# First block's norm from feature-major x, the product chain opened ahead of the second value tiles, and weights split once and reloaded

## The chip, the core and the metric

The kernel runs on one core of one Trainium2 chip. The metric is device time in microseconds for one execution. The profile is of one execution, taken by the hardware profiler. PE is TensorE's matmul queue, PEld its weight loads, DVE is VectorE, ACT is ScalarE, POOL is GpSimd and SP is SyncE, whose queue issues nearly all DMAs here.

## The reference, cut to what matters

One layer of a hybrid encoder trunk over 2048 tokens of width 1024. A norm, one wide input projection, three groups of heads that read it (a banded softmax attention, an mLSTM and a gated linear attention, GLA), an output projection, a residual and a final norm.

```python
hn = rmsnorm(x, norm_g)                      # x * rsqrt(mean(x*x) + eps) * g
z = jnp.einsum('bsd,de->bse', hn, w_in)      # 1024 -> 4252 columns, split by group:
# aq ak av ag | mq mk mv mo mi mf mg | gq gk gv ga gg
y_a = band_chunk_attention(aq, ak, av, rel_bias) * silu(ag)
h_ml = mlstm_chunkwise(silu(conv(mq)), silu(conv(mk)), mv, mi + b_i, mf + b_f)
y_b = sigmoid(mo) * head_rmsnorm(h_ml, ml_norm_g) * silu(mg)
log_alpha = log_sigmoid(ga @ w_alpha + b_alpha) / 16
y_c = head_rmsnorm(gla_chunkwise(gq, gk, gv, log_alpha), gla_norm_g) * silu(gg)
x = x + concat(y_a, y_b, y_c) @ w_out        # then the final rmsnorm
```

Inside GLA the score of a token t against an earlier token j of its chunk is `sum_d q[t,d] * k[j,d] * exp(b[t,d] - b[j,d])`, with b the running sum of log_alpha: the decay differs by key channel.

## The kernel before, in words

**Two phases.** Phase A goes through the sequence in four blocks of 512 tokens (`for q in range(NQ)`, L753). For each block it makes all input projections, the mLSTM and the GLA; the q, k, v and gate of the attention, and the finished parts of y, go to DRAM scratch. Phase B (from L783) does the attention and the output projection. In phase B only the four last `a` projections of block 3, kept back by `proj_a` (L504), have to do with the change.

**Split products.** Each projection is done with numbers split in two: a high part, rounded to a 32-bit matmul format, and the remainder as low part. A tile pair of 128 contraction rows takes three matmuls, high by high, high by low and low by high (L243 to L245, L263 to L265). x is split once a block by `split_x` (L323, ACT L329 and DVE or POOL L330) into eight tiles `X[k]`. Weights are split each time that they are used, by `load_w` (L229): the raw tile (0.5 MB, two buffers `wraw`) is loaded from DRAM (L233), ACT rounds it (L235), and DVE or POOL subtracts (L236; every third goes to POOL, `other()` L128). The split tile, 1 MB, goes into a ring of five (`wring`, L138). A block uses 33 of them: 25 of feature-major projections (`proj_f`, 24 matmuls each, one weight) and 8 of the two value projections (`proj_t`, 96 matmuls and four weights each).

**The order of the work.** The order on TensorE is that in which the program is written (`manual_schedule`, L132); the other engines and the SP queue are ordered ahead of time by the framework's scheduler, and each works through its list in order. `high_priority(offset=AHEAD)` moves instructions forward in that scheduler. To fill TensorE's waits, the program weaves chains into the projections: `Flow` (L33) keeps a clock in microseconds; a chain is a generator that yields (its TensorE time, a pause); after every half of a projection (`flow.piece(12 * 0.227)`) each chain whose pause is over takes one step. `flow.need(name)` steps the chains until that one is finished, and emits no projection meanwhile.

**One block, in order** (L753 to L778): `proj_z` makes the GLA's q and k (gq, gk); `proj_v` makes the first value tiles, calls `proj_gg` for the GLA's gate, and then makes the second value tiles; `need("gates")`; the chains `gla_in` and `gla` start (L761, L762); `proj_m` makes the six mLSTM q and k tiles; the chain `mlstm` starts; `proj_gm` makes the mLSTM's gates; then, if there is a next block, `need("gla_in")` (L771), and the chain `prep` for the next block starts; `proj_a` makes the attention's tiles; `need("prep")`, `split_x`, and the chain `gates` of the next block starts.

**The chains.** `gates` (L334): gate rows, log-sigmoids, scans (DVE L349, L353), then the transposed rows `rt` and, last, the row `iwl` (L391). `gla_in` (L621): for each half of the block, exponentials of the decay sums, and then the products of each token with the earlier ones in its group of 16, on POOL (L649 scales, L652 multiplies into four buffers `prd`), summed over channels by matmuls that write the bank `pw` (L658); so four products, then PE, then four more. `gla` (L665): L688 to L692 and L709 to L716, the norm, and the transposes L739. `mlstm` (L520): for each of four chunks L531, L541 to L545, L559 to L576, the norm on POOL and DVE (L595 to L601), a pause of 9 us, a wait until the gates `gm` exist, the transposes L610, and the result to DRAM.

**The norm of x.** `prep_x` (L281) loads the block's four row-major tiles of x, squares them on ACT with a sum per row (L287), and makes the scale of each token: mean plus epsilon on DVE (L288), the power -0.5 on POOL (L289), and four diagonal matrices on DVE (L292). `prep` (L295) spreads the scale over all partitions by a matmul with ones (L299), copies it to SBUF (L301), loads the four feature-major tiles of x (L305), scales them on DVE (L308) and makes the gate inputs (L315, L320). For the first block both run before any projection (L748 to L751), after 14 warm-up matmuls (L154) and beside the making of constants (L174 to L213: the `zr` lines fill `hl_nm`, `hl_iw` and `sel`).

Of the kernel before, what the change touches and what calls it, by code (L numbers as in the profile page):

```python
# [16 lines left out]
P = 128  # L17
# [10 lines left out]
G0 = 96  # L28

# [70 lines left out]
def f32(ap):  # L100
    return ap.bitcast(FP32)
# [3 lines left out]
def trunk_kernel(ctx: ExitStack, tc: tile.TileContext, xT, x, w_f, w_t, w_o, w_gates, norm_g, conv_w,  # L105
# [11 lines left out]
    y_d = dram.tile([NQ, P, KT, QT], FP32, name="y_d")  # L117

# [9 lines left out]
    def other():  # L128
        turn["n"] += 1
        return nc.gpsimd if turn["n"] % 3 == 0 else nc.vector  # L130
# [11 lines left out]
    with ExitStack() as pa_:  # L142
# [6 lines left out]
        def bank(tag, n=1):  # L149
            return (psum_i if tag == "ip" else psum).tile([P, 512], FP32, name=tag, bufs=n)  # L150
# [5 lines left out]
        def d_tile():  # L156
            return big.tile([P, 6, L], FP32, name="dd", bufs=1)
# [17 lines left out]
        zr = d_tile()  # L175
        nc.gpsimd.memset(zr, 0.0)
        nc.vector.tensor_copy(hl_nm, zr.rearrange("p h t -> p (h t)")[:, 0:QT])
        nc.vector.tensor_copy(hl_iw, zr[:, 0, 0:NC])
        nc.gpsimd.affine_select(out=zr[0:32], in_=zr[0:32], pattern=[[-1, 6], [0, P]], compare_op=ALU.not_equal,
                                fill=1.0, base=0, channel_multiplier=1)  # L180
        nc.scalar.copy(zr[32:64], zr[0:32])
        nc.scalar.copy(zr[96:128], zr[0:32])
        nc.vector.memset(zr[0:32], 0.0)
        nc.vector.tensor_copy(sel, zr)
# [44 lines left out]
        def load_w(src, k):  # L229
            w = wring.tile([P, 2 * D], FR, name="w").rearrange("p (k l n) -> p k l n", k=k, l=2)  # L230
            with tc.high_priority(offset=AHEAD):
                raw = wraws.tile([P, D], FP32, name="wraw")
                nc.sync.dma_start(raw, src)  # L233
                rv = raw.rearrange("p (k n) -> p k n", k=k)
                nc.scalar.copy(w[:, :, 0, :], rv)  # L235
                other().tensor_tensor(w[:, :, 1, :], rv, f32(w[:, :, 0, :]), op=ALU.subtract)  # L236
            return w

        def proj_g(name, X, out_, per):
            w = load_w(w_f[_F.index(name)], KT)  # L240
            ps = bank("ip", 2)
            for k in range(KT):
                nc.tensor.matmul(ps, w[:, k, 0, :], X[k][:, 0, :], start=(k == 0), stop=False)  # L243
                nc.tensor.matmul(ps, w[:, k, 0, :], X[k][:, 1, :], start=False, stop=False)  # L244
                nc.tensor.matmul(ps, w[:, k, 1, :], X[k][:, 0, :], start=False, stop=(k == KT - 1))  # L245
                if k % per == per - 1:
                    yield
            out_.append(ps)
# [7 lines left out]
        def proj_t(j, X, evac):  # L256
            ws = [load_w(w_t[j, g], 2) for g in range(4)]
# [37 lines left out]
        def prep(q, R, dg):  # L295
            t0 = q * QT
            yield 0.0, 0.0
# [23 lines left out]
            R["raws"], R["g1"] = raws, g1  # L321

# [197 lines left out]
        def mlstm(q, qk, vs, R):  # L520
            rt, iwl = R["rt"], R["iwl"]
            for c in range(NC):
# [81 lines left out]
                yield 1.7, 9.0  # L604
# [16 lines left out]
        def gla_in(q, z, ls_all, G):  # L621
            NB = ST // 16
            for sub in range(2):
# [124 lines left out]
        flow.start("prep", prep(0, R, prep_x(0)))  # L748
        load_consts()
        flow.finish("prep")  # L750
        X = split_x(R["raws"])  # L751
        flow.start("gates", gates(0, R["g1"], R))
        for q in range(NQ):  # L753
# [3 lines left out]
            z = proj_z(X)  # L757
            vs, vg, gg = proj_v(X, lambda: proj_gg(X))
            flow.need("gates")
            G = {}  # L760
            flow.start("gla_in", gla_in(q, z, R["ls"], G))  # L761
# [349 lines left out]
```

## Time and profile before

| | us |
|---|---|
| three runs | 1397.63, 1402.09, 1406.93 |
| median | 1402.09 |
| the profiled execution | 1396.99 |
| its span, from the first instruction to the last | 1395.3 |
| PE busy in the span | 1308.3 |
| POOL busy | 609.2 |
| mean granted clock of TensorE | 0.958 |

The first projection matmul (L243) starts at 32.3 us. Block 0 lasts to about 270 us, blocks 1 and 2 about 240 us each; phase B starts at about 972 us. A stage row gives a stretch of time, its length, and the busy time (and number of instructions) of PE, PEld, DVE, ACT, POOL, then the granted clock, the busy share of the DMA engines and GB/s. A timeline row gives start, busy time, engine, line, operation, out and in, and in brackets the idle time before it and what ended it. A wait row gives who waited for whom, the total in us, how often, and the longest.

### The profile page before, as it was taken

The page shows a single profiled execution, that of the slowest core. Times are in us where ns is not written, and L with a number is a line of the kernel's source. Part 1 is how long each engine was busy: PE and PEld are TensorE (multiplying, and loading weights), DVE is VectorE, ACT ScalarE, POOL GpSimd, SP SyncE. Part 2 cuts the span into 40 slices and gives each one's busy share as a digit, 9 for nine tenths or more (in the row PEclk, how much of TensorE's full clock was granted, in tenths as well). Part 3 has the DMA queues.
Part 4 walks back from the last instruction along what each step waited for, and adds up shares of the span by engine and source line. Part 5 has one row for each costly group of instructions (what it writes and reads, how often), then busy time and mean ns, then how long its engine had stood idle before and what let it go on. Part 6 is the DMA issues. An engine that isn't in the chain of part 4 may idle for free.

```text
span 1395.3 us, 20018 instructions
## 1 busy us (share of the span) xinstructions
PE 1308.3 (94%) x7044; PEld 1060.7 (76%) x7044; DVE 809.1 (58%) x1886; ACT 602.4 (43%) x1149; POOL 609.2 (44%) x847
## 2 busy tenths in 40 slices
PE   4999999999998999999899999997968999999997
PEld 2787778788777878877688787886857877877876
DVE  7626566562856556474556547555657756756731
ACT  5634322563432365343135434221566645645631
POOL 4225752431665234277322526631354453453452
PEclk7999999999998999999899999996969999999999
DMA  7444224534322463422233542231596654554222
GB/s 247 141 134 135 76 71 140 190 114 136 106 77 66 135 236 90 142 87 81 75 106 117 144 151 91 82 110 49 164 274 182 183 157 149 164 170 153 78 76 84
DMA packets 107205, 180.10 MB, mean 129 GB/s; under 512 B 9824, under 2 KB 54752, under 8 KB 107104
## 3 DMA queue, kind: packets, MB, share of 16 engines
q1 hardware_dynamic: 102496, 170.43, 40.2%
q10 hardware_dynamic: 4608, 8.39, 1.6%
q8 instruction: 56, 0.92, 0.3%
q14 instruction: 45, 0.37, 0.1%
HBM read 143.14 MB, written 35.65 MB: 128 GB/s over the span
## 4 chain that ended last, share of the span: by engine, by line
PE 72%; DVE 11%; DMA 5%; ACT 4%; POOL 3%; issue 3%; SPq 1%; POOLq 0%; DVEq 0%; ACTq 0%
PE ip L243 12%; PE ip L245 11%; PE ip L244 11%; PE ip L263 3%; PE ip L265 3%; PE ip L264 3%; PE s L860 3%; PE ip L984 3%; PE ip L982 3%; PE ip L983 3%; PE tp L924 2%; DVE pt L874 2%; PE ga L692 2%; PE w L941 2%; DMA wraw<-in_w_o 2%
## 5 line engine op out<-in xcount | busy, mean ns | idle before, releaser
L243 PE MATMUL ip<-x,w 128*128 128x512 f32 x800 | 329.5, 412 | 0.0
L245 PE MATMUL ip<-x,w 128*128 128x512 f32 x800 | 314.4, 393 | 0.0
L244 PE MATMUL ip<-x,w 128*128 128x512 f32 x800 | 313.8, 392 | 0.0
L243 PEld LDWEIGHTS ip<-x,w 128*128 128x128 f32 x800 | 151.3, 189 | 45.6 <-issue 15.9
L245 PEld LDWEIGHTS ip<-x,w 128*128 128x128 f32 x800 | 151.3, 189 | 33.9
L244 PEld LDWEIGHTS ip<-x,w 128*128 128x128 f32 x800 | 151.8, 190 | 30.0 <-issue 2.6
L236 POOL TENSOR_TENSOR w<-wraw,w 128x1024 fp32r<-128x1024 f32 x44 | 106.2, 2413 | 149.1 <-ACT w L235 149.1
L235 ACT CAST w<-wraw 128x1024 fp32r<-128x1024 f32 x132 | 138.1, 1047 | 60.5 <-DMA wraw<-in_w_t 25.3
L236 DVE TENSOR_TENSOR w<-wraw,w 128x1024 fp32r<-128x1024 f32 x88 | 119.5, 1358 | 76.4 <-ACT w L235 74.9
L879 POOL TENSOR_SCALAR pt<-pt,sm 128x640 f32<-128x640 f32 (+2 forms) x96 | 70.5, 736 | 147.9 <-DVE sm L878 116.9
L982 PE MATMUL ip<-wo,y 128*128 128x512 f32 x256 | 106.7, 417 | 0.0
L263 PE MATMUL ip<-w,x 128*128 128x512 f32 x256 | 100.4, 392 | 3.6 <-ACT vg L426 3.5
L877 ACT ACTIVATE pt<-pt,sm 128x640 f32<-128x640 f32 (+2 forms) x96 | 73.3, 763 | 69.8 <-DVE sm L874 67.4
L984 PE MATMUL ip<-wo,y 128*128 128x512 f32 x256 | 101.4, 396 | 0.3 <-POOL y L890 0.3
L983 PE MATMUL ip<-wo,y 128*128 128x512 f32 x256 | 101.2, 395 | 0.0
L265 PE MATMUL ip<-w,x 128*128 128x512 f32 x256 | 99.7, 389 | 0.0
L264 PE MATMUL ip<-w,x 128*128 128x512 f32 x256 | 99.6, 389 | 0.0
L930 DVE TENSOR_TENSOR pl<-tp,ph 128x512 fp32r<-128x512 f32 (+2 forms) x126 | 74.6, 599 | 32.0 <-ACT ph L929 30.7
L860 PE MATMUL s<-kk,qq 128*128 128x384 f32 (+1 forms) x360 | 80.9, 334 | 12.4 <-DVE sm L874 10.7
L652 POOL TENSOR_TENSOR prd<-gk,zg 128x16 f32<-128x16 f32 (+15 forms) x128 | 72.2, 564 | 31.1 <-PE pw L658 24.5
L860 PEld LDWEIGHTS s<-kk,qq 128*128 128x128 f32 x360 | 60.6, 201 | 31.3 <-DVE sm L874 25.0
L929 ACT CAST ph<-tp 128x512 fp32r<-128x512 f32 (+2 forms) x126 | 63.0, 509 | 34.1 <-PE tp L924 33.3
(244 smaller groups left out, 2413.9 us busy)
## 6 DMA issues: line engine op xcount, KB each, us to landing
wraw<-in_w_f SPq DMA_DIRECT2D x100, 512.0 KB, 3.6
wraw<-in_w_t SPq DMA_DIRECT2D x32, 512.0 KB, 3.7
qq<-q_d SPq DMA_DIRECT2D x48, 256.0 KB, 4.3
kk<-k_d SPq DMA_DIRECT2D x18, 512.0 KB, 6.3
vv<-v_d SPq DMA_DIRECT2D x18, 512.0 KB, 7.1
xraw<-in_x SPq DMA_DIRECT2D x16, 512.0 KB, 5.0
xraw<-in_xT SPq DMA_DIRECT2D x16, 512.0 KB, 6.4
xr<-in_x SPq DMA_DIRECT2D x16, 512.0 KB, 3.7
```

The costliest lines, as they stand in the source:

```text
L235: nc.scalar.copy(w[:, :, 0, :], rv)
L236: other().tensor_tensor(w[:, :, 1, :], rv, f32(w[:, :, 0, :]), op=ALU.subtract)
L243: nc.tensor.matmul(ps, w[:, k, 0, :], X[k][:, 0, :], start=(k == 0), stop=False)
L244: nc.tensor.matmul(ps, w[:, k, 0, :], X[k][:, 1, :], start=False, stop=False)
L245: nc.tensor.matmul(ps, w[:, k, 1, :], X[k][:, 0, :], start=False, stop=(k == KT - 1))
L263: nc.tensor.matmul(ps, X[k][:, 0, t], w[:, 0, :], start=(k == 0), stop=False)
L264: nc.tensor.matmul(ps, X[k][:, 0, t], w[:, 1, :], start=False, stop=False)
L265: nc.tensor.matmul(ps, X[k][:, 1, t], w[:, 0, :], start=False, stop=(k == KT - 1))
L860: nc.tensor.matmul(sp[:, :cn], qq[:, l, tt * P:(tt + 1) * P], kk[:, ko + c0:ko + c0 + cn], start=(l == 0), stop=(l == 1))
L982: nc.tensor.matmul(ps, Y[k][:, 0, t], wo[k, j][:, 0, :], start=(e == 0), stop=False)
L983: nc.tensor.matmul(ps, Y[k][:, 0, t], wo[k, j][:, 1, :], start=False, stop=False)
L984: nc.tensor.matmul(ps, Y[k][:, 1, t], wo[k, j][:, 0, :], start=False, stop=(e == KT - 1))
```

## The change

It has three parts.

1. *First block.* `prep_first` takes the place of `prep_x(0)`, `prep(0)`, `split_x` and `proj_z` of block 0. It loads only the feature-major x, squares it on ACT, adds the two tiles of a pair on DVE, sums over partitions by one-column matmuls, makes the scale as before, and spreads it per 128 tokens into a PSUM bank that the scaling reads. The order on ACT, DVE, POOL and SP is fixed by `keep_in_program_order`. The loads of x, gq and gk are first on the SP queue; the constants' loads and the `zr` lines come later (`late_consts`). The products of gq and gk are ordered so that all that need only the high part of x come first; the gate inputs come between them and the rest.
2. *The chain.* `gla_in` starts after `proj_gg`, ahead of the second value tiles, and polls until `iwl` exists. `need("gates")` moves behind `proj_m`, `need("gla_in")` in the block goes, and `prep` polls until `gla_in` is over. The pause of the last mlstm chunk's result becomes 17 us in blocks 0 to 2.
3. *The weights.* `load_w` stores each split tile (1 MB) to DRAM scratch when it is first made; every later use loads the split tile back, with no raw tile, rounding or subtraction.

```diff
+    w_d = [dram.tile([P, 2 * D], FP32, name=f"w_d{i}") for i in range(len(_F) + 8)]
...
+        def load_w(src, k, i):
+            flat = wring.tile([P, 2 * D], FR, name="w")
+            w = flat.rearrange("p (k l n) -> p k l n", k=k, l=2)
             with tc.high_priority(offset=AHEAD):
+                if i in made:
+                    nc.sync.dma_start(f32(flat), w_d[i])
+                    return w
                 raw = wraws.tile([P, D], FP32, name="wraw")
                 nc.sync.dma_start(raw, src)
                 rv = raw.rearrange("p (k n) -> p k n", k=k)
                 nc.scalar.copy(w[:, :, 0, :], rv)
                 other().tensor_tensor(w[:, :, 1, :], rv, f32(w[:, :, 0, :]), op=ALU.subtract)
+            made.add(i)
+            nc.sync.dma_start(w_d[i], f32(flat))
             return w
...
         def prep(q, R, dg):
-            yield 0.0, 0.0
+            while "gla_in" in flow.chains:
+                yield 0.0, 1.0
...
+        def prep_first():
+            pin = tc.keep_in_program_order
+            with tc.high_priority(offset=2 * AHEAD):
+                for g in range(4):
+                    raw = xraws.tile([P, 2, QT], FP32, name="xraw")
+                    pin(nc.sync.dma_start(raw, xT[:, 2 * g:2 * g + 2, 0:QT]))
...
+                for g in range(4):
+                    sq = sqs[:, 2 * (g % 3):2 * (g % 3) + 2, :]
+                    pin(nc.scalar.activation(sq, raws[g], AF.Square))
+                    pin(nc.vector.tensor_tensor(sq[:, 0, :], sq[:, 0, :], sq[:, 1, :], op=ALU.add))
+                    for tt in range(NC):
+                        nc.tensor.matmul(ss[:, tt:tt + 1], sq[:, 0, tt * P:(tt + 1) * P], ones[:, 0:1], ...)
+                pin(nc.vector.tensor_scalar(rs, ss[:, 0:NC], 1.0 / D, EPS, op0=ALU.mult, op1=ALU.add))
+                pin(nc.gpsimd.tensor_tensor(rs, rs, mhalf[:, 0:NC], op=ALU.pow))
...
+                for tt in range(NC):
+                    pin(nc.vector.tensor_scalar(dg[:, tt, :], ident, rs[:, tt:tt + 1], None, op0=ALU.mult))
+                    nc.tensor.matmul(rb[:, tt * P:(tt + 1) * P], ones, dg[:, tt, :], start=True, stop=True)
...
+                for (w, wr), n in zip(ws, ("gq", "gk")):
+                    pin(nc.scalar.copy(w[:, :, 0, :], wr))
+                    pin(nc.gpsimd.tensor_tensor(w[:, :, 1, :], wr, f32(w[:, :, 0, :]), op=ALU.subtract))
+                    nc.sync.dma_start(w_d[8 + _F.index(n)], f32(w).rearrange("p k l n -> p (k l n)"))
...
+                for k in range(KT):
+                    pin(nc.vector.scalar_tensor_tensor(rk[k], rk[k], ng[:, k:k + 1], rb, op0=ALU.mult, op1=ALU.mult))
+                    last = [pin(nc.scalar.copy(X[k][:, 0, :], rk[k])).ins, None]
+                for k in range(KT):
+                    op = pin((nc.gpsimd if k in LO_POOL else nc.vector).tensor_tensor(X[k][:, 1, :], rk[k], f32(X[k][:, 0, :]), op=ALU.subtract))
...
+            load_consts()
+            late_consts(last)
...
-                yield 1.7, 9.0
+                yield 1.7, 9.0 if c < NC - 1 or q == NQ - 1 else 17.0
...
-        def gla_in(q, z, ls_all, G):
+        def gla_in(q, z, R, G):
             NB = ST // 16
+            while "iwl" not in R:
+                yield 0.0, 1.0
...
+            z = proj_z(X) if q else z
             G = {}
-            flow.start("gla_in", gla_in(q, z, R["ls"], G))
+
+            def between():
+                g = proj_gg(X)
+                flow.start("gla_in", gla_in(q, z, R, G))
+                return g
+
+            vs, vg, gg = proj_v(X, between)
             flow.start("gla", gla(q, vg, gg, G))
             flow.need("mlstm")
             if q + 1 < NQ:
                 dg = prep_x(q + 1)
             qk = proj_m(X)
+            flow.need("gates")
...
             if q + 1 < NQ:
-                flow.need("gla_in")
                 R = {}
                 flow.start("prep", prep(q + 1, R, dg))
```

More of the change, by code (lines that the diff above doesn't have):

```diff
@@ L28 @@
 G0 = 96
+LO_POOL = (4, 7)
+LO_ORDER = (0, 1, 2, 3, 5, 6, 4, 7)
 class Flow:
@@ L174, in trunk_kernel @@
         hl_iw = one.tile([P, NC], FR, name="hl_iw")
[L175 to L184, printed above, removed]
         cap = one.tile([P, L], FP32, name="cap")
@@ L226, in load_consts @@
             nc.vector.tensor_scalar(glg, glg, 0.5, None, op0=ALU.mult)
-        def load_w(src, k):
-            w = wring.tile([P, 2 * D], FR, name="w").rearrange("p (k l n) -> p k l n", k=k, l=2)
+        made = set()
+        def load_w(src, k, i):
+            flat = wring.tile([P, 2 * D], FR, name="w")
+            w = flat.rearrange("p (k l n) -> p k l n", k=k, l=2)
             with tc.high_priority(offset=AHEAD):
+                if i in made:
+                    nc.sync.dma_start(f32(flat), w_d[i])
+                    return w
                 raw = wraws.tile([P, D], FP32, name="wraw")
@@ L256, in proj_t @@
         def proj_t(j, X, evac):
-            ws = [load_w(w_t[j, g], 2) for g in range(4)]
+            ws = [load_w(w_t[j, g], 2, 4 * j + g) for g in range(4)]
             for tt in range(NC):
@@ L321, in prep, with late_consts @@
             R["raws"], R["g1"] = raws, g1
+        def late_consts(last):
+            zr = d_tile()
+            nc.gpsimd.memset(zr, 0.0)
+            with tc.issue_after(last[1]):
+                nc.vector.tensor_copy(hl_nm, zr.rearrange("p h t -> p (h t)")[:, 0:QT])
+            with tc.issue_after(last[1]):
+                nc.vector.tensor_copy(hl_iw, zr[:, 0, 0:NC])
+            nc.gpsimd.affine_select(out=zr[0:32], in_=zr[0:32], pattern=[[-1, 6], [0, P]], compare_op=ALU.not_equal,
+                                    fill=1.0, base=0, channel_multiplier=1)
+            with tc.issue_after(last[0]):
+                nc.scalar.copy(zr[32:64], zr[0:32])
+            with tc.issue_after(last[0]):
+                nc.scalar.copy(zr[96:128], zr[0:32])
+            with tc.issue_after(last[1]):
+                nc.vector.memset(zr[0:32], 0.0)
+            with tc.issue_after(last[1]):
+                nc.vector.tensor_copy(sel, zr)
@@ L619, in trunk_kernel @@
         b16 = lambda t: t.rearrange("p (b i) -> p b i", i=16)
-        def gla_in(q, z, ls_all, G):
+        def gla_in(q, z, R, G):
             NB = ST // 16
+            while "iwl" not in R:
+                yield 0.0, 1.0
+            ls_all = R["ls"]
             for sub in range(2):
@@ L747, in trunk_kernel @@
         R = {}
[L748 to L752, printed above, removed]
+        g1, X, z = prep_first()
+        flow.start("gates", gates(0, g1, R))
         for q in range(NQ):
@@ L756, in trunk_kernel @@
             flow.need("gla")
-            z = proj_z(X)
-            vs, vg, gg = proj_v(X, lambda: proj_gg(X))
-            flow.need("gates")
+            z = proj_z(X) if q else z
             G = {}
-            flow.start("gla_in", gla_in(q, z, R["ls"], G))
+            def between():
[3 more added lines that the diff above has]
+            vs, vg, gg = proj_v(X, between)
             flow.start("gla", gla(q, vg, gg, G))
```

52 lines of the change are left out of this document (51 added, 1 removed).

## The prediction

> **What bounds the kernel now.** I read the page first: engine shares, the sliced PE and clock rows, the chain that ended last.
>
> ```profile
> PE 1308.3 (94%) x7044; PEld 1060.7 (76%) x7044; DVE 809.1 (58%) x1886; ACT 602.4 (43%) x1149; POOL 609.2 (44%) x847
> ...
> PEclk7999999999998999999899999996969999999999
> ...
> PE 72%; DVE 11%; DMA 5%; ACT 4%; POOL 3%; issue 3%; SPq 1%; POOLq 0%; DVEq 0%; ACTq 0%
> ```
>
> TensorE is the bound nearly everywhere. Only the places where it isn't can pay, and the dips of the clock row point at them. A table by stage (us; then busy time of PE, PEld, DVE, ACT, POOL; granted clock, DMA share, GB/s) has the stages cut where the matmuls of the projections stop and start again:
>
> ```profile
> 0.00:32.30 32.30, 14.50 (x46) 7.47 (x46) 23.21 (x53) 17.89 (x25) 16.98 (x27) 0.74 0.76 252
> ...
> 179.90:194.10 14.20, 11.48 (x86) 8.86 (x85) 9.56 (x25) 4.21 (x9) 12.83 (x25) 0.76 0.26 75
> ...
> 418.00:433.80 15.80, 11.90 (x86) 8.69 (x85) 8.81 (x22) 4.21 (x9) 13.47 (x24) 0.68 0.19 54
> ...
> 654.50:671.00 16.50, 11.80 (x85) 8.92 (x84) 9.97 (x26) 4.21 (x9) 13.46 (x25) 0.79 0.20 53
> ...
> 937.20:971.70 34.50, 24.66 (x164) 22.44 (x163) 21.01 (x67) 5.70 (x13) 8.12 (x19) 0.71 0.14 36
> ```
>
> So there are five holes: the start, three equal stretches of 14.2, 15.8 and 16.5 us in which TensorE issues only some 86 small matmuls while POOL is the busy engine (12.8 to 13.5 us), and the end of the first phase. The three are the line that drains the product chain, `flow.need("gla_in")`, L771: nothing of the projections may be issued until the last products (POOL L649/L652) are summed (PE L658). What TensorE waited for between 32 and 937 us says the same, and names the rest:
>
> ```profile
> PE pw L658 <- POOL prd L652: 6.2, 5, 1.8
> PE mt L610 <- DVE m L601: 5.4, 2, 3.7
> ...
> PE ip L263 <- ACT vg L426: 3.5, 3, 2.0
> ```
>
> No projection matmul waited for a weight tile in that list.
>
> **Part 1, the first block.** Landings, single steps and the first matmuls in the order of time:
>
> ```profile
> 4.38 1.04 ACT L235 CAST w<-wraw 128x1024 fp32r<-128x1024 f32 x1 [2.31 <-DMA wraw<-in_w_f]
> ...
> 5.69 1.04 ACT L235 CAST w<-wraw 128x1024 fp32r<-128x1024 f32 x1 [0.26 <-DMA wraw<-in_w_f]
> ...
> 8.84 1.06 ACT L287 ACTIVATE xraw<-xraw 128x1024 f32<-128x1024 f32 x1 [2.10 <-DMA xraw<-in_x]
> ...
> 15.22 1.03 POOL L289 TENSOR_TENSOR rs<-rs,mhalf 128x4 f32<-128x4 f32 x1 [4.27 <-DVE rs L288]
> ...
> 16.29 0.87 DVE L292 TENSOR_SCALAR g<-ident,rs 128x128 f32<-128x128 f32 x4 [1.15 <-POOL rs L289]
> ...
> 27.67 1.28 DVE L330 TENSOR_TENSOR x<-xraw,x 128x512 fp32r<-128x512 f32 x2
> ```
> ```profile
> 17.30 2.04 PE L299 MATMUL pw<-g,ones 128*128 128x512 f32 x2 [10.36 <-DVE g L292]
> ...
> 32.32 0.50 PE L243 MATMUL ip<-x,w 128*128 128x512 f32 x1
> ```
> ```profile
> 44.20 0.39 PE L245 MATMUL ip<-x,w 128*128 128x512 f32 x1
> ...
> 45.11 0.39 PE L263 MATMUL ip<-w,x 128*128 128x512 f32 x1
> ```
>
> The two first weight loads land 1.31 us apart, 0.524 MB each: 400 GB/s. Four matmul starts lie between 44.20 and 45.11, so a projection matmul costs 0.2275 us. The first value tile starts at 45.11.
>
> Removed: four row-major x loads ahead of four more of feature-major x, and the wait between the two. In the new order the four feature-major loads are first on the SP queue: landed at 4.4, 5.7, 7.0, 8.3, and gq and gk at 9.6 and 10.9. Then in a row: last square 1.06, pair sum 0.64 (half of the L330 row), four one-column matmuls about 1, rs 0.2, the power on POOL 1.03, the diagonals 0.87, the broadcast about 1 at half clock (half of L299's 2.04, since it overlaps the diagonals), and 1 for seven handovers: 15.1. The first scaled tile and its rounding make the first product start near 16.7 instead of 32.32. DVE then sets the pace: the eight scalings at their mean,
>
> ```profile
> L308 DVE SCALAR_TENSOR_TENSOR xraw<-xraw,ng,g 128x512 f32<-128x512 f32 x32 | 27.5, 921 | 3.4 <-ACT g L301 3.4
> ```
>
> 7.4 us to 22.5, six low parts at 0.64 to 26.3; two on POOL. PE follows: 24 products end near 24, eight more (1.8), the gate matmuls (about 2), sixteen low-part products (3.6): the value tiles start at 31.2, with 1.5 added for a half clock that catches the first products 32.7. Before, two gate matmuls (about 0.9) lay ahead of 45.11 that now come later. Gain 45.1 - 0.9 - 32.7 = 11.5. Bounds: 15 (no clock loss, scalings at half a L330 pair), 6 (the value weights are late: both raw tiles are held by gq and gk until POOL has subtracted, near 17 us, and the third and fourth weight need two more rounds of load, cast and subtract).
>
> The Trainium skill, "SBUF — State Buffer", section "Who interferes with whom", says that a DVE instruction with two SBUF inputs and a GpSimd instruction that reads SBUF exclude each other for a whole instruction, and that one with a single SBUF input is free of it. The new scalings read the row scale from PSUM, so by this rule they would run at their fastest beside POOL's subtractions and the start would gain about 1.4 us more; the sum above keeps the mean row.
>
> **Part 2, the product chain opened ahead of the second value tiles.** The chain now starts after the gg projections, one value projection earlier, or as soon as the gates' last step is emitted, and L771 goes; `prep` polls instead, while the `a` projections run on. The second value projection and two neighbouring sums of the chain:
>
> ```profile
> 81.80:103.50 21.70, 21.70 (x97) 18.00 (x96) 5.29 (x9) 6.07 (x13) 3.92 (x2) 1.00 0.39 109
> ```
> ```profile
> 119.98 0.64 PE L658 MATMUL pw<-prd,hs 128*32 128x256 f32 x8
> 131.66 0.42 PE L658 MATMUL pw<-prd,hs 128*32 128x80 f32 x8
> ```
>
> The start moves by 21.7 us. The chain has eight groups 11 to 12 us apart, some 92 us; from the end of gg (81.8) to that of gm (179.9) are 98 us, so it ends before gm does and the polling costs nothing. If it had to poll, `prep` (its own pauses sum to about 15 us) would come later inside nine `a` projections of 5.46 us.
>
> The small matmuls of the three holes stay and must be paid at full clock. How long they take there shows at the end of the phase, where the same groups still run at full clock:
>
> ```profile
> 937.16 0.27 PE L688 MATMUL gb<-ident,dr 128*128 128x128 f32 x1
> ...
> 939.14 0.87 PE L531 MATMUL s<-hl_nm,sel 128*128 128x128 f32 x6
> 940.66 0.67 PE L709 MATMUL ga<-Sbd,q 128*128 128x256 f32 x2 [0.66 <-DVE at L702]
> ...
> 944.11 0.94 PE L559 MATMUL s<-Cbd,qk 128*128 128x130 f32 x6 [0.34 <-DVE dd L553]
> ...
> 971.21 0.87 PE L610 MATMUL mt<-ident,m 128*128 128x128 f32 x3 [5.14 <-DVE m L601]
> ```
>
> L688 to L531 2.85, L709 to L559 3.45, three groups of L658 1.2 to 1.9: 7.5 a hole. Gain 46.5 - 22.5 = 24. Lower bound by busy time times clock (11.48 x 0.76 + 11.90 x 0.68 + 11.80 x 0.79 = 26.1): 20.4. Upper 25.5. The slow matmuls just behind the third hole are another 1.5 (0 to 1.7).
>
> The longer pause of the last mlstm chunk (9 to 17 us of flow time) is meant for L610, which waited 5.4 us for L601: gain 5 (0 to 5.4). At the end of the phase gla is now 22 us further on, so its matmuls move from the hole under projections; but the hole is mlstm's own chain (L531 to L610, 14.4 us a chunk at the last), which stays. I take 3 (8 to -1). The clock stays low there.
>
> **Part 3, weights split once.** Removed in blocks 1 to 3: 99 of 132 casts and subtractions,
>
> ```profile
> L236 POOL TENSOR_TENSOR w<-wraw,w 128x1024 fp32r<-128x1024 f32 x44 | 106.2, 2413 | 149.1 <-ACT w L235 149.1
> L235 ACT CAST w<-wraw 128x1024 fp32r<-128x1024 f32 x132 | 138.1, 1047 | 60.5 <-DMA wraw<-in_w_t 25.3
> L236 DVE TENSOR_TENSOR w<-wraw,w 128x1024 fp32r<-128x1024 f32 x88 | 119.5, 1358 | 76.4 <-ACT w L235 74.9
> ```
>
> about 104 us of ACT, 90 of DVE, 80 of POOL. All of it lay beside TensorE, so it is worth only the evacuation waits it caused (L263 for L426, 3.5 us, and small ones): 2 (0 to 6). Added: 33 stores of 1.05 MB in block 0, 99 reloads of 1.05 MB for 0.52 MB.
>
> ```profile
> 45.10:282.90 237.80, 230.67 (x1241) 185.22 (x1240) 139.91 (x285) 97.81 (x166) 103.16 (x157) 0.99 0.39 121
> ```
> ```profile
> wraw<-in_w_f SPq DMA_DIRECT2D x100, 512.0 KB, 3.6
> ```
>
> Block 0 moves 237.8 x 121 = 28.8 MB; with the stores 63.4 MB, 158 us at 400 GB/s, or 204 at 310 (121 over its share of 0.39), of some 225: it fits, tightly. Supply of one weight in block 0: load 3.6, 2.6 behind one store, cast 1.05, subtract 1.36 or 2.41 (mean 1.7), handovers 0.4: 9.3 us through two raw tiles, 4.7 a weight against 24 x 0.2275 = 5.46 of PE. I take 4 us lost (0 to 15: two stores ahead of each load make 6.0 a weight, 0.5 late thirty times). Reloads take 2.6 + 2.3 = 4.9 us and five tiles stand ahead: 1.5 lost (0 to 10; the place is a value projection, which holds four of the five). If the cover is gone, each late weight is paid in full, since TensorE has nothing else queued in order.
>
> **Sum.** 11.5 + 24 + 1.5 + 5 + 3 + 2 - 4 - 1.5 = 41.5 from the profiled execution's own 1396.99 (span 1395.3 and 1.7 around it): **1355**. That execution is 5 us below the median shown, 1402.09, at the low edge of the runs; I forecast 1355 and let the range take the 5.
>
> **Rivals.**
> *Stores crowd block 0.* For: 91% of the DMA time by the lower rate, and the supply margin is 0.8 us a weight. Against: 400 GB/s was reached when loads stood in line. Lost 20 instead of 4: 1371. The Trainium skill, "DMA: Bandwidth & Descriptors", section "Queues, rings and completion order", has descriptors consumed in ring order on each engine, so a load behind a store waits for all of it; two stores in line are then this rival.
>
> *The SP queue is held, slower.* SP issues in order; a reload needs TensorE to free its tile, and stands among stores that wait for late evacuations:
>
> ```profile
> SPq L495 <- DVE hl L493: 94.9, 12, 22.2
> ...
> SPq L419 <- DVE hl L417: 52.5, 15, 5.1
> ```
>
> Three quarters of both (blocks 1 to 3) are 110 us. Where the ring has no spare tile this comes through; if 75 us of it do, 1355 + 75 = 1430. It decides once a hold is longer than the cover: 5 x 5.46 - 4.9 = 22 us in `a` projections (longest hold 22.2), but under 1 us in value projections. Against: these holds exist today, in front of loads too, and no weight was late.
>
> *The hole only moves.* The chain is still unfinished at gm's end, since it needs the gates' last step too, and `prep`, the gates and the next block's first products wait: half the 24 is lost, 1367.
>
> *More than that.* Bounds on the good side (start 15, evacuations 6, end 8, no store cost): 1335.
>
> **How the numbers follow.** Forecast 0.62, crowded stores 0.12, hole moves 0.09, more 0.10, SP held 0.04, and 0.03 that the parts cancel (1395, no change). Own range of the likeliest 1342 to 1368; with the neighbours 1336 to 1382 holds 8 in 10. A measurement here tells about 1% (14 us): faster below 1388: 0.91; within 0.04; slower 0.05.
>
> **What would show it.** Right: first product near 17 us and first value matmul near 33; no stretch without projection matmuls near 170 to 180, 400, 630, and the clock row at 9 there; PE no longer waiting for L652 there; L235 with 33 executions; 33 x 1.05 + 99 x 0.52 = 86 MB more by DMA, block 0 at about 280 GB/s. Wrong: projection matmuls that wait for a weight's DMA or for L236, SP waits for stores in front of reloads, or an end of the first phase that is longer than 34.5 us.

## The result and the profile after

| | after | before, beside it |
|---|---|---|
| median | 1365.11 us | 1400.95 us |
| lowest and highest | 1362.99, 1367.44 | |
| ratio, 95% interval | 0.9758 [0.9733, 0.9783] | |
| profiled execution, span | 1365.31, 1363.6 | 1396.99, 1395.3 |

The kernel is 2.4% faster. The forecast was 1355, with 1336 to 1382 as its range: the sign and the main mechanism hold, and 10 us of the sum do not. Which terms gave more and which less, the stages show.

In the changed kernel the lines have new numbers: L244 to L246 are the feature-major projections (before L243 to L245), L264 to L266 the value projections (L263 to L265), L232 loads a raw weight, L234 and L235 round and subtract, L237 stores the split tile, L229 reloads it, L699 and L708 are the last mLSTM steps (L601 and L610). `vg L524` and `zg L415` are evacuations, copies of a finished bank out of PSUM. In the runs of the experiments the same lines stand a few numbers off: in `raws`, for example, L233 loads a raw weight and L235 rounds it.

From the page of the changed kernel: engine shares, the clock by slices, the bytes moved.

```profile
PE 1297.1 (95%) x7094; PEld 1056.6 (77%) x7094; DVE 702.0 (51%) x1825; ACT 508.2 (37%) x1044; POOL 523.4 (38%) x814
...
PEclk7999999999999999999999999997958989999999
...
DMA packets 111379, 264.50 MB, mean 194 GB/s; under 512 B 10288, under 2 KB 55216, under 8 KB 94384
```

The two dips that the clock row of before had between the start and the end of the first phase (slices 13 and 20, where the second and third hole lay) are gone: it reads 9 from the second slice to the 27th. TensorE's share of the chain that ended last goes from 72% to 78%.

The stages of the changed kernel, in the columns of the earlier table (stretch; length, busy time of PE, PEld, DVE, ACT, POOL; clock, DMA share, GB/s). They are cut at the first value matmul of block 0, the start of gg, the first mLSTM tile, the first value matmuls of blocks 1 to 3, and around the last hole.

```profile
0.00:37.80 37.80, 30.40 (x144) 24.84 (x144) 24.43 (x60) 18.24 (x23) 16.68 (x27) 0.82 0.63 210
37.80:68.00 30.20, 25.90 (x100) 19.77 (x101) 12.96 (x29) 18.68 (x35) 7.43 (x14) 0.94 0.90 356
68.00:107.10 39.10, 35.74 (x164) 27.94 (x163) 20.23 (x44) 14.94 (x26) 14.90 (x13) 1.00 0.78 273
107.10:275.80 168.70, 168.70 (x982) 135.69 (x980) 102.78 (x202) 67.91 (x112) 83.33 (x126) 1.00 0.78 276
275.80:502.90 227.10, 227.02 (x1250) 183.36 (x1249) 105.81 (x274) 61.39 (x128) 71.75 (x145) 1.00 0.55 200
502.90:729.60 226.70, 226.70 (x1250) 183.39 (x1249) 103.90 (x264) 60.21 (x123) 72.49 (x145) 1.00 0.52 185
...
910.70:938.70 28.00, 15.55 (x109) 13.82 (x108) 15.69 (x48) 3.71 (x6) 5.25 (x11) 0.76 0.12 31
```

The same cuts in the kernel before, for its first value tiles and its two middle blocks:

```profile
45.10:70.00 24.90, 22.64 (x100) 18.07 (x99) 20.98 (x52) 16.73 (x32) 9.14 (x20) 1.00 0.20 56
...
282.90:521.40 238.50, 232.00 (x1249) 186.36 (x1248) 140.90 (x285) 95.60 (x165) 105.36 (x157) 0.98 0.38 118
521.40:764.20 242.80, 234.41 (x1249) 188.78 (x1249) 139.06 (x286) 92.62 (x157) 102.85 (x155) 0.97 0.34 103
```

With the same 1249 or 1250 matmuls, blocks 1 and 2 went from 238.5 and 242.8 us to 227.1 and 226.7, and TensorE is busy through them without a gap. The new first stretch is 7.3 us shorter, but the first value tiles, up to the start of gg, take 30.2 us instead of 24.9, with the DMA engines at a share of 0.90.

What TensorE waited for between 32 and 905 us in the changed kernel:

```profile
PE ip L264 <- ACT w L234: 2.8, 1, 2.8
PE ip L244 <- ACT vg L524: 2.6, 1, 2.6
PE ip L244 <- DMA w<-w_d: 1.6, 1, 1.6
PE ip L265 <- DVE w L235: 1.5, 2, 0.8
...
PE ip L264 <- DMA w<-w_d: 0.8, 1, 0.8
```

The waits for POOL's products and for the mLSTM's m are no longer in it. New are waits for weights: L234 and L235 in the first block, and two reloads (1.6 and 0.8 us, both in block 3).

Where the time went, from the starts of the same matmuls in both traces (us):

| point | before | after | after minus before |
|---|---|---|---|
| first product | 32.32 | 22.95 | -9.4 |
| first value matmul | 45.11 | 37.86 | -7.3 |
| first mLSTM tile | 103.56 | 107.17 | +3.6 |
| block 1, first value matmul | 282.90 | 275.79 | -7.1 |
| block 2 | 521.45 | 502.93 | -18.5 |
| block 3 | 764.22 | 729.59 | -34.6 |
| third projection matmul behind the last hole | 972.74 | 939.73 | -33.0 |
| span | 1395.3 | 1363.6 | -31.7 |

About 1.5 us of the +3.6 are small matmuls of the chain that now stand ahead of that point. Read by differences: the early gain of 9.4 us is not only lost by the first mLSTM tile but turned round, by 13; the rest of block 0, block 1 and block 2 bring 10.7, 11.4 and 16.1; block 3 with the last hole, and phase B, bring nothing (+1.6, +1.3).

### The profile page after: what moved, and what is told of

It is laid out like the page before. It is cut to its first block, busy times and chain, and to the rows that moved or that the text cites. A ratio compares the mean times of both kernels' runs of the same rounds, so it can differ in the third digit from the quotient of the medians.

```text
span 1363.6 us, 19920 instructions
## 1 busy us (share of the span) xinstructions
PE 1297.1 (95%) x7094; PEld 1056.6 (77%) x7094; DVE 702.0 (51%) x1825; ACT 508.2 (37%) x1044; POOL 523.4 (38%) x814
## 2 busy tenths in 40 slices
DMA packets 111379, 264.50 MB, mean 194 GB/s; under 512 B 10288, under 2 KB 55216, under 8 KB 94384
## 4 chain that ended last, share of the span: by engine, by line
PE 78%; DVE 8%; DMA 5%; ACT 3%; issue 3%; POOL 2%; SPq 0%; POOLq 0%; DVEq 0%; ACTq 0%
PE ip L244 13%; PE ip L246 12%; PE ip L245 12%; PE ip L264 3%; PE ip L265 3%; PE ip L266 3%; PE s L962 3%; PE ip L1086 3%; PE ip L1085 3%; PE ip L1084 3%; PE tp L1026 2%; DVE pt L976 2%; PE ga L793 2%; PE w L1043 2%; DMA kk<-k_d 1%
## 5 line engine op out<-in xcount | busy, mean ns | idle before, releaser
L244 PE MATMUL ip<-x,w 128*128 128x512 f32 x784 | 320.8, 409 | 4.2 <-ACT vg L524 2.6
L246 PE MATMUL ip<-x,w 128*128 128x512 f32 x784 | 307.0, 392 | 0.0
L245 PE MATMUL ip<-x,w 128*128 128x512 f32 x784 | 306.4, 391 | 0.0
L244 PEld LDWEIGHTS ip<-x,w 128*128 128x128 f32 x784 | 147.6, 188 | 46.4 <-issue 13.5
L246 PEld LDWEIGHTS ip<-x,w 128*128 128x128 f32 x784 | 147.4, 188 | 32.6
L245 PEld LDWEIGHTS ip<-x,w 128*128 128x128 f32 x784 | 147.9, 189 | 28.4 <-issue 1.7
L264 PE MATMUL ip<-w,x 128*128 128x512 f32 x256 | 103.0, 403 | 4.7 <-ACT w L234 2.8
L265 PE MATMUL ip<-w,x 128*128 128x512 f32 x256 | 100.9, 394 | 2.2 <-DVE w L235 1.5
L266 PE MATMUL ip<-w,x 128*128 128x512 f32 x256 | 100.4, 392 | 0.0
L495 ACT ACTIVATE e<-ip 128x512 f32<-128x512 f32 x44 | 26.3, 597 | 168.4 <-PE ip L246 168.4
L565 DVE SCALAR_TENSOR_TENSOR qk<-u,cw,qk 128x512 f32<-128x512 f32 x72 | 61.2, 850 | 42.8 <-ACT qk L563 41.1
L786 POOL TENSOR_TENSOR Kt<-lc,Dt 128x16 f32<-128x16 f32 (+6 forms) x112 | 41.4, 394 | 71.9 <-PE ga L793 44.4
```

What stands on the lines that cost most here:

```text
L264: nc.tensor.matmul(ps, X[k][:, 0, t], w[:, 0, :], start=(k == 0), stop=False)
L265: nc.tensor.matmul(ps, X[k][:, 0, t], w[:, 1, :], start=False, stop=False)
L266: nc.tensor.matmul(ps, X[k][:, 1, t], w[:, 0, :], start=False, stop=(k == KT - 1))
```

## The experiments

**Theories.** *Late value weights*: the new start is lost again in the first value tile, because its weights arrive late; either the stores to DRAM delay them (*stores*), or the raw tiles that gq and gk hold until POOL has subtracted (*raw tiles*), or the slow diagonals ahead of both (*lock*: while POOL runs one of its instructions, a DVE instruction of some kinds can't run beside it). *Pause*: it is worth the 5 us of the prediction, or nothing. *Reload*: it costs a little, as forecast, or it brings time by relieving the other engines. Results, each with the kernel before run beside it:

| run | us | before | ratio, 95% | first product | first mLSTM tile |
|---|---|---|---|---|---|
| part1 | 1391.56 | 1398.87 | 0.9952 [0.9930, 0.9973] | 22.92 | 100.32 |
| part2 | 1364.63 | 1398.87 | 0.9756 [0.9730, 0.9782] | 31.89 | 105.00 |
| part3 | 1390.95 | 1398.87 | 0.9945 [0.9930, 0.9961] | 33.09 | 102.99 |
| parts12 | 1367.91 | 1398.87 | 0.9779 [0.9750, 0.9808] | 22.91 | 102.72 |
| parts23 | 1356.93 | 1398.19 | 0.9718 [0.9694, 0.9742] | 34.01 | 104.75 |
| diag | 1369.09 | 1398.19 | 0.9799 [0.9775, 0.9822] | 19.36 | 108.97 |
| late | 1359.35 | 1398.19 | 0.9731 [0.9710, 0.9752] | 22.68 | 101.16 |
| pause | 1383.31 | 1398.19 | 0.9903 [0.9881, 0.9926] | 22.45 | 106.10 |
| raws | 1354.20 | 1399.68 | 0.9675 [0.9650, 0.9701] | 23.26 | 101.52 |
| raws_diag | 1358.90 | 1399.68 | 0.9703 [0.9675, 0.9730] | 20.24 | 99.89 |
| raws_diag_late | 1361.29 | 1399.68 | 0.9721 [0.9697, 0.9745] | 20.39 | 101.01 |
| raws_diag_late_x | 1355.62 | 1399.68 | 0.9679 [0.9651, 0.9708] | 20.65 | 99.31 |

### One part at a time

Each run makes the named part of the change and leaves the rest as before.

```diff
 # part1
+        g1, X, z = prep_first()
+        flow.start("gates", gates(0, g1, R))
 # part2
+            vs, vg, gg = proj_v(X, between)
-                flow.need("gla_in")
+                yield 1.7, 9.0 if c < NC - 1 or q == NQ - 1 else 17.0
 # part3
+                if i in made:
+                    nc.sync.dma_start(f32(flat), w_d[i])
+                    return w
```

> The kernel before with the new first block alone. My theory: the first value matmul comes some 7 us earlier (before 45.1, all three parts 37.9), and without the stores of the split tiles the value weights are not late, so the gain is still there at the first mLSTM tile (before 103.6): 96 to 98 there and 1394 to 1396 in all. Rival: it is the raw tiles held by gq and gk that make the value weights late, stores or not: 102 to 104 at the first mLSTM tile and no change in the total (1400 to 1402).

Part 1 alone brings 7.3 us. Its first product comes at 22.92, 9.4 earlier, but at the first mLSTM tile only 3.2 are left, and at block 3 it is 0.9 behind the kernel before; the gain of the span appears in phase B (417.6 us instead of 422.6), which the part doesn't touch and where the granted clock was 0.96 instead of 0.94 in the two executions profiled. So neither theory's number came out: the start itself gives away two thirds within 100 us even without stores, and the 5 us of phase B are not shown to come from the part.

> The kernel before with the product chain opened early alone. My theory: this part makes nearly the whole gain of the three: the stretches without projections near 180, 418 and 655 us go, 1365 to 1371. Rival (the relief of ACT, DVE and POOL by the reloads is what made blocks 1 to 3 shorter than forecast): at most 24 us, 1377 or more.

Part 2 alone brings 34.2 us, as much as all three parts together. What TensorE waited for between 32 and 905 us in it:

```profile
PE ip L272 <- ACT vg L436: 4.0, 3, 2.1
PE pw L671 <- POOL prd L665: 0.6, 1, 0.6
```

Of the chain's waits 0.6 us are left; evacuations (vg) are the largest remaining wait.

> The kernel before with the weights split once and reloaded alone. My theory: block 0 loses 3 to 6 us to the stores, blocks 1 to 3 gain 0 to 3, the three stretches without projections stay: 1400 to 1406. Rival (relief): blocks 1 to 3 gain 8 to 12, 1390 to 1396.

Part 3 alone brings 7.9 us where the theory of the prediction had it cost a little. Block 1 starts 2.8 us later than before (its first product is already 0.8 later), so the stores do cost something in block 0, but the first phase then ends 5.9 us earlier: the relief of ACT, DVE and POOL is worth more than stores and reloads cost.

The three single gains sum to 49.5 us; joined, they gave 35.8 (1400.95 to 1365.11). Some 14 us are missing. About 5 of them are the phase B of part 1; for the rest the pairs show where the parts meet.

### Two parts at a time

Part 3 left out, then part 1 left out.

> All but the split tiles' stores and reloads: every weight is split anew at each use. My theory (stores crowd block 0): the first mLSTM tile starts at 97 to 100 instead of 107.2, blocks 1 to 3 keep their length within 3 us, 1356 to 1361 in all. Rival (relief): blocks 1 to 3 become 8 to 12 us longer and the total is 1366 to 1372.

> All but the new first block: the old norm and the old order of the first block, with the early chain and the reloads. If the new first block gains nothing in the joined kernel, because what it gains at the first product is gone by the first mLSTM tile (107.2 with all three, 105.0 with the early chain alone): first mLSTM tile at 104 to 106, total 1359 to 1365. Rival, that the first block is worth its forecast and something else costs it: 1370 or more.

Without stores the compressed start reaches the first mLSTM tile at 102.7 instead of 107.2: the stores cost 4.5 us there. But blocks 1 and 2, with casts and subtractions back, take 229.2 and 232.1 us instead of 227.1 and 226.7, so the total is 1367.9. With stores but the old first block, that tile comes at 104.75, no later than in part 2 alone (105.00): **stores hurt the first value tiles only where the start is compressed**. Between 32 and 905 us TensorE waits there 1.2 us for evacuations and 0.4 us for a reload.

At 1356.9, some 8 us below the full change and below what either theory had, parts 2 and 3 alone are the better kernel by the medians. The intervals of the two ratios (up to 0.9742, from 0.9733) overlap by a little, and in the profiled executions 4.9 us of it are there when the last hole ends (933.87 instead of 938.73); the rest is phase B. So part 1 as written gains nothing in the joined kernel, and is probably a net loss.

### The diagonals on ACT

The start of the changed kernel in the order of time, power, subtraction, diagonals, broadcast, raw loads, scalings and the first product:

```profile
10.06 1.06 ACT L361 ACTIVATE qk<-xraw 128x1024 f32<-128x1024 f32 x1 [1.13 <-DMA xraw<-in_xT]
...
14.04 1.03 POOL L368 TENSOR_TENSOR rs<-rs,mhalf 128x4 f32<-128x4 f32 x1 [6.88 <-DVE rs L367]
...
15.04 4.64 POOL L380 TENSOR_TENSOR w<-wraw,w 128x1024 fp32r<-128x1024 f32 x2
15.11 5.04 DVE L374 TENSOR_SCALAR g<-ident,rs 128x128 f32<-128x128 f32 x4 [0.78 <-POOL rs L368]
...
17.78 0.43 SPq L232 DMA_DIRECT2D wraw<-in_w_t  x1
...
20.07 0.51 SPq L232 DMA_DIRECT2D wraw<-in_w_t  x1
...
22.95 0.80 PE L398 MATMUL ip<-x,w 128*128 128x512 f32 x1 [0.21 <-ACT x L387]
```

The fourth x tile was squared from 10.06 on, not 8.3: a small constant's load went first on SP, the first x tile landed at 5.2 instead of 4.4, and the fourth landed 2.1 us behind the third instead of 1.3. The last one-column matmuls took 1.86. And the four diagonals, 0.87 us before, took 5.04: about as long as POOL's two subtractions (4.64) that begin beside them. Taken one by one, the first diagonal lasts as long as POOL's first subtraction, the second as long as its second, and the other two, behind both, are as short as before:

```profile
15.04 2.34 POOL L380 TENSOR_TENSOR w<-wraw,w 128x1024 fp32r<-128x1024 f32 x1
15.11 2.35 DVE L374 TENSOR_SCALAR g<-ident,rs 128x128 f32<-128x128 f32 x1 [0.78 <-POOL rs L368]
...
19.68 0.47 DVE L374 TENSOR_SCALAR g<-ident,rs 128x128 f32<-128x128 f32 x2
```

These rows show the lock. The value weights' raw loads (17.78, 20.07) follow the end of each subtraction. The edit moves the diagonals to ACT:

```diff
-pin(nc.vector.tensor_scalar(dg[:, tt, :], ident, rs[:, tt:tt + 1], None, op0=ALU.mult))
+pin(nc.scalar.activation(dg[:, tt, :], ident, AF.Copy, scale=rs[:, tt:tt + 1]))
```

> All three parts, with the four diagonals of the first block made on ACT, so that they do not stand on DVE while POOL subtracts gq and gk (they took 5.04 us there instead of 0.87). Theory of the exclusive lock between DVE and POOL: the first product starts at 18.5 to 19.5 instead of 22.95, the first value matmul at 33 to 35. If the value weights then decide (their loads wait for the raw tiles, not for the products), gg starts within 1.5 us of 68.1 and the total stays at 1362 to 1366; if they don't, the whole 4 us come through: gg at 64 and 1360 to 1361.

```profile
15.34 1.28 ACT L374 ACTIVATE g<-ident,rs 128x128 f32<-128x128 f32 x4 [4.63 <-POOL rs L368]
...
17.62 4.75 POOL L380 TENSOR_TENSOR w<-wraw,w 128x1024 fp32r<-128x1024 f32 x2 [2.32 <-ACT w L379]
17.90 5.36 DVE L386 SCALAR_TENSOR_TENSOR xraw<-xraw,ng,gb 128x512 f32<-128x512 f32 x8 [3.57 <-PE gb L375]
```

On ACT the diagonals take 1.28 us and the first product starts at 19.36, 3.6 earlier: that is the price of the lock at this place. (They are through before POOL begins at 17.62, so this run doesn't show how ACT and POOL go side by side.) The kernel isn't faster for it (1369.1, above both expectations). The subtractions now begin 2.6 us later, so the raw tiles come free later, and TensorE waits longer for the value weights; gg starts at 65.94, 2.1 earlier, and the first mLSTM tile at 108.97, 1.8 later than in the change:

```profile
PE ip L264 <- ACT w L234: 5.5, 2, 3.9
PE ip L265 <- POOL w L235: 1.8, 2, 1.4
```

So the diagonals were on the path to the first product, and not on the path to the end.

### Stores put off, and raw tiles of their own

What the first value tiles of the changed kernel waited for (subtraction, load, cast, matmul):

```profile
31.92 3.02 DVE L235 TENSOR_TENSOR w<-wraw,w 128x1024 fp32r<-128x1024 f32 x2
...
33.16 0.33 SPq L232 DMA_DIRECT2D wraw<-in_w_t  x1
33.54 0.42 SPq L237 DMA_DIRECT2D w_d<-w  x1
34.97 0.53 SPq L232 DMA_DIRECT2D wraw<-in_w_t  x1
...
39.06 1.05 ACT L234 CAST w<-wraw 128x1024 fp32r<-128x1024 f32 x1 [1.25 <-DMA wraw<-in_w_t]
...
45.77 1.04 ACT L234 CAST w<-wraw 128x1024 fp32r<-128x1024 f32 x1
...
46.87 0.50 PE L264 MATMUL ip<-w,x 128*128 128x512 f32 x1 [2.84 <-ACT w L234]
```

The third and fourth weight need the raw tiles of the first two. Those were cast by 27.8 and 29.3, but DVE, busy with x until then, subtracted them only from 31.92 to 34.94. So the third weight's load is issued at 33.16 and cast at 39.06; the fourth, issued at 34.97 behind a store, is cast only at 45.77, and TensorE waits 2.84 us for it. Two edits take away one cause each. `late` stores the tiles of gq, gk, gg and the value projections in block 1, which splits them once more, instead of block 0:

```diff
+LATE = [8 + e for e, n in enumerate(_F) if n[0] in "ma"]
...
+            if st["q"] > 0 or i in LATE:
+                made.add(i)
+                nc.sync.dma_start(w_d[i], f32(flat))
```

> All three parts, but gq, gk, gg and the value tiles are stored when block 1 splits them again, not in block 0: so no store stands among the first loads. If stores delay the value weights: the wait of 2.8 us for a rounded value weight near 44 to 47 us goes, the first mLSTM tile starts at 102 to 104, the total is 1360 to 1364. If the two raw tiles alone delay them: 106 to 107 and 1364 to 1367.

`raws` keeps all stores, and gives gq's and gk's raw weights the space of tiles that aren't in use yet, so that the value weights' raw loads go out right behind them:

```diff
+for n, held in (("gq", big.tile([P, 2, QT], FP32, name="gg", bufs=1)), ("gk", big.tile([P, 3, QT], FP32, name="gm", bufs=1))):
+    ...
+    wraw = held.rearrange("p a t -> p (a t)")[:, 0:D]
...
+with tc.issue_after(st["gk"]):
+    nc.sync.dma_start(raw, src)
```

> All three parts, with gq's and gk's raw tiles in the still unused space of gg and gm, so that the two raw buffers of the value weights are free from the start (their first two loads come right behind gk's). If the held raw tiles make the value weights late: the waits for a rounded weight between 41 and 47 us go, gg starts at 62 to 64 instead of 68.1, the first mLSTM tile at 101 to 103, total 1359 to 1361. If the crowd of stores and of block 1's x loads on the DMA engines makes them late: the third and fourth value weight still land after 40 us, gg at 66 to 68, total 1363 to 1366.

Either helps. `late` brings the first mLSTM tile to 101.2, `raws` to 101.5, six us earlier than the change. In total `late` gives 0.9731 [0.9710, 0.9752], whose interval still touches that of the change; `raws` gives **0.9675 [0.9650, 0.9701], 1354.2 us**, clear of it, the fastest here and some 5 us below its theory. In `raws` the value weights are issued at 4.44 and the first of them is cast at 13.48, some 24 us before the first value matmul at 39.1:

```profile
4.44 0.93 SPq L233 DMA_DIRECT2D wraw<-in_w_t  x2
...
13.48 1.04 ACT L235 CAST w<-wraw 128x1024 fp32r<-128x1024 f32 x1 [0.24 <-DMA wraw<-in_w_t]
```

and the stretch from the first value matmul to the start of gg is 23.7 us with TensorE busy in all of it, where the change needs 30.2:

```profile
39.10:62.80 23.70, 23.68 (x101) 18.92 (x102) 13.29 (x21) 17.44 (x30) 7.73 (x14) 1.00 0.78 295
```

So the lateness has two parts: raw tiles that are held, by POOL's subtractions first and DVE's after them, which push the third and fourth load behind 33 us, and the stores that then stand in the same queue. Taking away either is enough for the first mLSTM tile.

The total of `raws` holds more than this. Of the 8.5 us between the two profiled executions, 5.7 are there at the first mLSTM tile, 5.3 at block 1 and 3.2 at the end of the last hole (935.57 instead of 938.73). The other 5.3 fall in phase B, whose text is the same, at a granted clock of 0.96 instead of 0.94. And the interval of `raws` overlaps that of `parts23` (0.9694 to 0.9742): that the mended new start gains over the old one is not shown.

### What is left of the start

`raws_diag` puts the diagonals on ACT as well, `raws_diag_late` also puts the stores off, `raws_diag_late_x` also holds block 1's x loads behind the last value weight's:

```diff
+with tc.issue_after(st["ld"]):
+    nc.sync.dma_start(xt, x[...])
```

> The same with the four diagonals on ACT. If the supply of weights bounds the first block, the 3.6 us that the products then start earlier (19.4 instead of 22.95) are lost again by the first mLSTM tile, and the total is that of the raw tiles' run within 2 us. If it doesn't, the total is 3 to 4 us under that run.

> The same, and gq, gk, gg and the value tiles stored in block 1 instead of block 0. If stores crowd the supply: no wait for a weight in block 0, gg at 57 to 59, first mLSTM tile at 95 to 97, total 1351 to 1355, under the early chain with reloads and the old first block (1356.9). If not: no more than 2 us under the run before it.

> The same, and block 1's loads of x (2 MB) held on the SP queue behind the last value weight of block 0. If those loads crowd the first weights too: another 1 to 3 us less. Rival: the weights then land in time already and the hold only delays the norm of block 1, 0 to 2 us more.

No more came of it. The first product moves to about 20.4 and the first mLSTM tile to 99.3 to 101.0, 0.5 to 2.2 us before `raws`, and the totals are 1358.9, 1361.3 and 1355.6: none below `raws`, though all three intervals overlap its own. `raws_diag` is 4.7 us above it where its theories had it within 2 us or below, and holding the x loads brought 5.7 us where 1 to 3 were expected. With raw tiles free, the stores cost nothing more that is seen here, and in `raws_diag` the start waits for the rounding of x (2.2 us) and for evacuations (1.8 us) instead.

Why the totals stand 1 to 7 us above `raws` isn't settled: the other engines and SP are ordered ahead of time by the scheduler, every edit reorders some of it, and phase B alone differed by up to 5 us between kernels whose phase B is the same text, at granted clocks between 0.94 and 0.96.

### The pause

The last mlstm chunk's pause back to 9 us, with all else as in the change:

```diff
-                yield 1.7, 9.0 if c < NC - 1 or q == NQ - 1 else 17.0
+                yield 1.7, 9.0
```

> All three parts with the old pause of 9 us behind the last mLSTM chunk. By the forecast the transposes of that chunk wait for their input again, some 5 us over the blocks: 1368 to 1371. Rival: without the drain that wait is not there, 1364 to 1366.

1383.3 us: the longer pause is worth 18 us, more than any theory had. TensorE's waits between 32 and 980 us, and DVE ahead of the first of them:

```profile
PE mt L708 <- DVE m L699: 27.4, 5, 8.1
```
```profile
285.05 0.69 DVE L458 TENSOR_TENSOR g<-g 6x512 f32<-6x512 f32 x1
...
286.00 0.55 DVE L688 TENSOR_REDUCE sm<-m 128x6 f32<-128x384 f32 x1
...
289.80 1.09 DVE L744 TENSOR_TENSOR Dt<-Dt,dl 128x10 f32<-128x10 f32 x7
...
293.34 0.56 DVE L699 TENSOR_TENSOR m<-m,sm 128x384 f32<-128x384 f32 x1 [1.78 <-POOL v L523]
```

Three of the five waits (8.06, 4.59 and 3.79 us, one at the head of each of blocks 1 to 3) are new; the other two belong to the end of the phase, where the change waits too. With the drain gone, the last chunk's norm (L688 to L699) comes while DVE works on the next block's gates (L458) and on `gla_in` (L744), step between step; its steps on POOL (289.7 to 293.3) stand between steps of `gla_in` there in the same way. L708 holds TensorE's whole queue until the norm is through.

## Why the prediction was right, and where it was not

The total was inside its range, and the three drains, the largest term, are what the change removed. That it came within 10 us is in part luck: the start came out 11 us worse than forecast and the end 5 us worse, the drains with the pause and the relief 7 us better. By the terms of its sum:

| term | forecast | measured |
|---|---|---|
| start, and stores in block 0 (to the first mLSTM tile) | -11.5 + 4 | +3.6 (+2.1 without the chain's own matmuls) |
| drains, slow matmuls, pause, relief, reloads (to block 3) | -31 | -38.2 |
| block 3 with the end of the first phase | -3 | +1.6 |
| phase B | 0 | +1.3 |
| sum | -41.5 | -31.7 |

- *What bounds the kernel.* Right: only the holes paid. All three drains went, the chain's polling cost nothing, and part 2 alone gave 0.9756. The signs on the DMA side came as named: weights were split 33 times, 84 MB more moved (264.50 instead of 180.10; 86 forecast), and block 0 ran at 273 to 276 GB/s (280).
- *The first block.* The step that failed. "Then in a row" priced the diagonals at 0.87 us from a trace in which POOL was free; beside POOL's subtractions of gq and gk they took 5.04. The first product came at 22.95 instead of 16.7: 1.8 of that by the x load, 4.2 by the lock. The Trainium skill, "SBUF — State Buffer", "Who interferes with whom", names `tensor_scalar` among the DVE operations that can take the port pair shared with GpSimd, and says that the one issued first keeps it for a whole instruction; the trace agrees (2.35 us for a diagonal beside POOL's subtraction of 2.34; 0.47 for two behind it). The prediction applied that section to the scalings alone. There too it agrees: with the row scale read from PSUM, eight of them took 5.36 us beside POOL in `diag`, 0.67 each, against a mean of 0.921 before: 2.0 us less for the eight, where the prediction named 1.4 without showing from what.
- *Its lower bound was the likely case.* "The value weights are late: both raw tiles are held by gq and gk until POOL has subtracted" stood there as the bound of 6 us. It happened, and was worse than the bound, since the loads then met the stores. `raws` takes this one cause away, and the first mLSTM tile starts 5.7 us earlier (11 us less in all, of which 5 are phase B).
- *Stores.* The rival that they crowd block 0 was wrong as it was put (thirty late weights through the block): from the first mLSTM tile to block 1 TensorE is busy for 168.7 of 168.7 us at a DMA share of 0.78. By `parts12` they cost 4.5 us, in one place, at the start. It was an interaction of two terms that the sum had as independent.
- *Pause.* The mechanism was right and the size was off: 5 us forecast, 18 measured. The 5.4 us was the wait in the old order, where the drain came ahead of the next block's work; the wait that the new order would have had can't be read from the old trace.
- *Relief.* 2 forecast, less 1.5 for reloads. On top of the early chain, reloading is worth 7.7 us without the new start (part2 and parts23, 1364.63 and 1356.93, of which the ratios' intervals, [0.9730, 0.9782] and [0.9694, 0.9742], overlap a little), and with it 2 and 5 us in blocks 1 and 2 (`parts12` against the change). Which engine's relief does it wasn't tested.
- *End of the phase.* The hole shrank by some 6.5 us, twice the forecast, but block 3 and the end together did not get shorter. The stretch from the first value matmul of block 3 to the hole, before and after:

```profile
764.20:936.90 172.70, 171.46 (x899) 138.43 (x898) 96.84 (x180) 65.73 (x114) 88.69 (x137) 1.00 0.38 114
729.60:910.50 180.90, 178.37 (x958) 144.05 (x957) 73.09 (x183) 44.67 (x96) 68.90 (x141) 1.00 0.56 196
```

The chain's matmuls did move under the projections, as the prediction says: 59 more stand here, and they take 6.9 us of TensorE. That is what the hole gave. The prediction priced such matmuls for the three drains (22.5 us) and put them at nothing here. Another 1.3 us are waits: two for reloads, 2.4 us in all, where before one for an evacuation took 1.2.
- *SP held.* The rival's mechanism exists and did little harm. The SP queue's own waits:

```profile
SPq L229 <- PE ip L246: 309.5, 55, 10.0
...
SPq L229 <- PE ip L266: 33.8, 16, 20.8
...
SPq L895 <- DVE hl_nm L462: 14.7, 1, 14.7
```

Reloads wait 310 us on SP for feature-major projections to free a ring tile, at most 10.0 us at a time, and 34 us for value projections, once for 20.8 (in block 1); none of these waits reached TensorE. What did reach it is the third row: in block 3 a load of phase B (L895) stood on SP from 730.15 to 744.90, waiting for DVE, and more loads of phase B followed. The next reload went out at 751.08, and two reloads came 1.6 and 0.8 us late.

## What to carry to other kernels

A duration from the old trace holds only for the neighbours that it had there: ask which engine stands beside each short step in the new order, DVE and POOL above all, and whether a stall was hidden by the very wait that the change removes. When a start is compressed, follow the buffers and not only the chain to the first product: here two buffers held until slow subtractions were through cost the joined kernel what the early start gave it, and putting gq's and gk's raw tiles in space that was idle anyway brought the first mLSTM tile forward by 5.7 us. Work that moves out of a hole must still be paid where it lands, if that place is bound by the same engine. Parts whose gains are measured alone (7, 34 and 8 us) may share a resource; run the pairs before keeping all three, and see by stages whether a gain falls where the edit is: 5 of part 1's 7 us did not.

## What was unexpected of the hardware

Two short waits close together halved TensorE's clock. In `diag`, TensorE idled 1.61 and 0.76 us before two matmuls:

```profile
85.41 0.50 PE L264 MATMUL ip<-w,x 128*128 128x512 f32 x1 [1.61 <-ACT w L234]
86.67 0.55 PE L265 MATMUL ip<-w,x 128*128 128x512 f32 x1 [0.76 <-DVE w L235]
87.02 0.63 PE L266 MATMUL ip<-w,x 128*128 128x512 f32 x1
```

From 87.02 the starts are 0.43 us apart instead of 0.23, and stay so until 93.8. The Trainium skill, "TensorE: Matmul & The Clock Gate", Part 1, gives an idle window of some 3.4 us as the condition; here the two idle times sum to 2.4 us, with a matmul between them. The length of a wait alone doesn't tell. A single one of 2.09 us in `part2` was followed by 3.4 us at half clock, and one of 2.59 us in the changed kernel by none:

```profile
57.78 0.50 PE L272 MATMUL ip<-w,x 128*128 128x512 f32 x1 [2.09 <-ACT vg L436]
76.27 0.50 PE L244 MATMUL ip<-x,w 128*128 128x512 f32 x1 [2.59 <-ACT vg L524]
```

(The granted clock is 0.51 from 58.4 to 61.9 us in `part2`, and 1.00 from 76.2 to 82 in the changed kernel.) What decides is not settled by these runs. A late operand in a stretch of projections thus costs its wait, and can cost more than that again in slow matmuls: in `diag` 6.8 us at half speed, 3.4 us lost for 2.4 us of waiting.
